# A one-layer hybrid encoder: query and key stores on ScalarE, fewer transfers of softmax statistics, operand sums on VectorE

## The chip, the cores and the metric

One Trainium2 chip, one of its cores. The metric is the device time of one execution in microseconds (us). Before the change three runs took 1313.45, 1315.63 and 1310.13 us, a median of 1313.45. A core has a matrix engine (TensorE, in the profile PE, with its weight loads as PEld), three engines for elementwise work (VectorE = DVE, ScalarE = ACT, GpSimd = POOL) and SyncE (SP), which here issues all transfers. Each engine works through its own list of instructions in order.

## The reference

One layer over x of 1024 positions by 1024 features, and 256 memory tokens, in float32. With `h = rms_norm(x)`, a single projection makes queries, keys and values of 8 heads of 64, a gated convolution input and the queries of 4 memory heads:

```python
q, k, v, glu, qm = split(rms_norm(x) @ w_in)
# group A: windows (128,1), (512,4), (2048,16): width and stride of the keys,
#          each normalised, then combined by the softmax of their log-sum-exps
# group B: GLU, depthwise convolution over 31, layer norm, silu
# group C: attention of qm to 256 memory tokens
h = x + concat(A, B, C) @ w_out
f = depthwise_conv3(rms_norm(h) @ w_up)          # 2 x 2816 columns
out = h + (silu(f_gate) * f_up) @ w_down
```

## The kernel before, in words

**Numbers.** A float32 operand is split into a high and a low part that TensorE takes (`hi`, `lo`); a product is three passes, hi*hi, hi*lo and lo*hi. ScalarE copies the high part, VectorE or GpSimd subtracts to get the low part.

**Stages of the span.** Until about 560 us the input projection (L917), the heads, the convolution, the memory heads and the output projection (L1099) run interleaved; from 562 to 622 the second norm, which also turns its rows into operands of the FFN's up projection; to 1064 the up projection in 22 pairs of column blocks, by a Strassen-like scheme with seven products over operands named A11, A12, A22, S1 to S4; to the end the down projection (L1334).

**Order of the work.** The program is written as generators (`Steps`) whose parts are started and advanced in turn; tiles come from pools with few buffers (`st.new`, `st.free`), and a scheduler with a model of the times sets the order of each engine's list. So an edit in one place can move rows elsewhere.

**Queries and keys.** `heads` (L829 on) takes a projected block of 128 positions by 256 columns out of PSUM (`raw`, L832, ScalarE), squares it (L833), norms it, splits it (`hl`, L864), has TensorE turn it (L871), copies it out of PSUM on ScalarE (`out`, L875) and stores it to DRAM through SP (L877): `qk_d` 32 times, the memory heads' `qm_d` 8 and `km_d` 2 times, 256 KB each. `values` (L884 to L890) stores the values in two orders, `v_d` by position (L888) and `vr_d` by class (L890). `head` (L338 on) loads `qk` (L346 to L349) and v (L393, L394) from there.

**Statistics.** Each head has two groups of scores: the near window, in which a block of 128 queries starts 64 positions late (so the last block wraps around, `qe`), and the class group, whose queries are gathered by position mod 64 into classes (`qc`), with masks m2a and m2b. For each query and group there is a maximum and a sum (`stat`, `stat2`). To combine the groups, `softmax_weights` brings the class group's statistics into the near group's order through DRAM: 8 stores to `st_d` (L299), 4 loads (L303 to L306), then weights on GpSimd and ScalarE, a turn on TensorE, and 4 stores to `w_d` (L336, L337); `weigh` loads the weights as rows, spread over 64 partitions (`wt`, L468), multiplies, adds and splits.

**Mixed parts.** The split result of each of the 8 column blocks of the mixed heads (k = 0 to 3 the heads, 4 and 5 the convolution, 6 and 7 memory) is kept in SBUF when its place is there (`mx`, `mx_more`, `mx_last`), and otherwise goes from `mx_part` to DRAM (`m_d`, L229) and back (L1085). Which of these it is depends on the moment at which the part is made: `room_for` (L206 on). The output projection takes the parts in the rounds 0, then 4 and 5, then 1, 2, 6, then 3 and 7. Convolution parts are made at L1024 (ScalarE) and L1026 (VectorE).

**The second norm.** `norm(t)` takes the eight row tiles of 128. VectorE scales (L1173, two halves). For tiles 4 to 7 the halves of tile t - 4 (`low0`, `low1`) and of tile t (`high0`, `high1`) are combined in place: `high1 = high0 + high1` on GpSimd (L1183, gives S1), `high0 = low0 - high0` (L1184, S3) and `low0 = high1 - low0` (L1185, S2) on VectorE, `low1 = low1 - low0` on GpSimd (L1189, S4). `turn_rows` turns each on TensorE (L1159, `ps_n`), copies the high part on ScalarE (L1161) and subtracts for the low part on VectorE (L1162). The FFN's first weights are loaded, summed (L1221) and split (L1207, L1208) at the same time, mostly on GpSimd. The first product of the up projection is `ps_d` at L1226.

Of the kernel before, what the change touches and what calls it, by code (L numbers as in the profile page):

```python
# [9 lines left out]
F = mybir.dt.float32  # L10
R = mybir.dt.float32r
I32 = mybir.dt.int32
AF = mybir.ActivationFunctionType
OP = mybir.AluOpType
# [4 lines left out]
S, D = 1024, 1024  # L19
# [24 lines left out]
def constants():  # L44


    c = {}
    n = np.arange(S)
# [9 lines left out]
    m2 = np.where(in4 & in16, twice, np.where(in4 | in16, np.float32(0), neg)).astype(np.float32)  # L58
    c["m2a"], c["m2b"] = m2[0:128], m2[128:256]
# [73 lines left out]
def block(tc, a, out):  # L133
# [3 lines left out]
    def f32(ap):  # L137
        return ap.bitcast(F)
# [38 lines left out]
    w_d = [dpool.tile([1, 2, S + 64], F, name=f"w_d{h}") for h in range(8)]  # L177
# [111 lines left out]
    def split_mixed(k, parts, src, cut=slice(None)):  # L289
        hi, lo = (t[:, cut] for t in parts)  # L290
        act.activation(natural(hi), classed(src), AF.Copy)
        yield
        dve.tensor_tensor(natural(lo), classed(src), f32(natural(hi)), OP.subtract)

    def softmax_weights(h, stat, stat2):


        for k in range(8):
            sp.dma_start(st_d[h][k].rearrange("(r s) c n -> s r (c n)", r=4),  # L299
                         stat2[16 * k : 16 * k + 16].rearrange("s r c n -> s r (c n)"))  # L300
        yield
        there = stat[:, 1].rearrange("p u c n -> p u (c n)")
        sp.dma_start(there[0:64], st_d[h][1:8:2].rearrange("k p c n -> p k (c n)"))  # L303
        sp.dma_start(there[64:128, 0:3], st_d[h][2:7:2].rearrange("k p c n -> p k (c n)"))
        for c in range(2):
            sp.dma_start(stat[64:128, 1, 3, c], st_d[h][0, :, 1 - c])  # L306
# [28 lines left out]
        for g in range(2):  # L335
            sp.dma_start(w_d[h][0, g, 64 : S + 64].rearrange("(u p) -> u p", p=128), rows[8 * g : 8 * g + 8])  # L336
            sp.dma_start(w_d[h][:, g, 0:64], rows[8 * g + 7 : 8 * g + 8, 64:128])  # L337
        count(("w", h))  # L338

    def head(h):  # L340
# [9 lines left out]
        for _ in range(3):  # L350
# [5 lines left out]
        pool.tensor_scalar(qc.rearrange("p r (k s) -> p r k s", s=16),  # L356
                           f32(q).rearrange("p (k r s) -> p r k s", r=4, s=16), 1.0, 0.0, OP.mult, OP.add)
# [43 lines left out]
        def evacuate(ps, j):  # L401

            other = yield from st.new("other", [128, 512])
            out, more = us[j // 2][to : to + 64], other[to : to + 64]
            if j < 2:
                n = 512 if j == 0 else 448
                views = [(out[:, 512 * j + 64 : 512 * j + 64 + n], ps[:, 0:n], more[:, 0:n])]
                if j:
                    views.append((out[:, 0:64], ps[:, 448:512], more[:, 448:512]))
            else:  # L410
                out = out.rearrange("p (k r s) -> p r k s", r=4, s=16)[:, 2 * j - 4 : 2 * j - 2]
                views = [(out, *(t.rearrange("p (r k s) -> p r k s", r=2, s=16) for t in (ps, more)))]
            act.activation(more, ps[frm : frm + 64], AF.Copy)
            for o, p, _ in views:
                act.activation(o, p[to : to + 64], AF.Copy)
            st.free("o")
            yield
            for o, _, m in views:
                pool.tensor_tensor(o, o, m, OP.add)
            st.free("other")  # L420
            count(("u", h))
            yield
# [33 lines left out]
    def weigh(p):  # L456
# [19 lines left out]
        for half in range(2):  # L476
# [10 lines left out]
            yield from split_mixed(p, parts, us[0][:, cut], cut)  # L487
# [73 lines left out]
    with tc.tile_pool(name="p1", bufs=1, side="right") as p1:  # L561
# [266 lines left out]
        def heads(ps, g, keys, rot, dst, key):  # L828
# [48 lines left out]
            sp.dma_start(dst, f32(t))  # L877
# [286 lines left out]
    def norm(t):  # L1164
# [18 lines left out]
        pool.tensor_tensor(high1, high0, high1, OP.add)  # L1183
# [5 lines left out]
        pool.tensor_tensor(low1, low1, low0, OP.subtract)  # L1189
# [177 lines left out]
```

## Time and profile before

| | us |
|---|---|
| runs (median of three) | 1313.45 |
| the profiled execution's own time | 1310.28 |
| its span | 1308.5 |
| TensorE busy | 1197.1 |
| VectorE, GpSimd, ScalarE busy | 868.7, 788.5, 626.6 |
| mean granted TensorE clock (of full speed) | 0.963 |

How to read its lines. A page gives busy time by engine, and the span in 40 slices of 32.7 us, a digit for each (tenths, 9 is 90% or more). A row of the timeline is start, duration, engine, line and operation with what it writes and reads, and in brackets the idle time of the engine ahead of it and what released it. A row of waits is who waited at which line, for what: us in total, times, longest. A row of the chain (start, duration, what) is a piece of the work that ended last, followed back. A row of a line's groups ends with minimum/median/maximum in ns and the first and last start in us. SPq is SP's queue, that is, the issuing of transfers, which isn't counted as busy time.

### The profile page before, as it was taken

To read this page: it belongs to the slowest core of one execution; us is meant where nothing else is said; L and a number is where in the kernel's file an instruction comes from. 1 tells how busy PE (TensorE), PEld (TensorE's weight loads), DVE (VectorE), ACT (ScalarE), POOL (GpSimd) and SP (SyncE) were. 2 spreads that over 40 slices of the span, in tenths; PEclk is the share of its full clock that TensorE was granted. 3 is DMA by queue.
4 is the path that set the end of the run, shared out by engine and by line. 5 is a ranking of instruction groups with operands and counts; after the bars stand their busy time and mean duration, and the time that the engine had idled before them with its cause. 6 is when DMAs were issued, how large, how long until landed. Compare 5 with 4: busy or idle time off the path is not lost.

```text
span 1308.5 us, 18556 instructions
## 1 busy us (share of the span) xinstructions
PE 1197.1 (91%) x6287; PEld 1000.3 (76%) x6287; DVE 868.7 (66%) x1272; ACT 626.6 (48%) x1296; POOL 788.5 (60%) x793
## 2 busy tenths in 40 slices
PE   4899988799988898885999999999999999999997
PEld 3887887799877786563877777777777788888886
DVE  6748879676685786887487778778787762224222
ACT  5664165468766576553344444344444443333331
POOL 4835286498894454367466667676676745555552
PEclk9999988999989898896999999999999999999999
DMA  7353525566575622161122222222222254448443
GB/s 253 112 170 100 159 82 161 169 180 178 144 252 164 188 74 78 28 213 49 34 87 81 65 86 67 81 89 65 89 71 83 81 175 155 145 145 272 146 146 120
DMA packets 166555, 164.81 MB, mean 126 GB/s; under 512 B 20322, under 2 KB 125756, under 8 KB 166460
## 3 DMA queue, kind: packets, MB, share of 16 engines
q1 hardware_dynamic: 166460, 163.63, 40.3%
q8 instruction: 49, 0.80, 0.3%
q14 instruction: 46, 0.38, 0.1%
HBM read 121.51 MB, written 42.08 MB: 125 GB/s over the span
## 4 chain that ended last, share of the span: by engine, by line
PE 46%; DVE 18%; issue 8%; ACT 7%; POOL 6%; DMA 5%; SPq 1%; POOLq 0%; ACTq 0%; DVEq 0%
PE ps_dn L1334 18%; PE ps_c L1226 6%; PE ps_d L1226 6%; PE proj L1099 4%; PE proj L917 3%; DVE yg L1295 3%; DVE conv L980 2%; DVE yu L1295 2%; PE o L287 2%; DMA v<-vr_d 2%; POOL up_lo L1208 2%; PE turn L278 2%; PE ps_a L1226 2%; ACT yu L1293 2%; DVE yg L1294 1%
## 5 line engine op out<-in xcount | busy, mean ns | idle before, releaser
L917 PE MATMUL proj<-w_hi,hnT 128*128 128x256 f32 x896 | 188.1, 298 | 23.7 <-ACT raw L832 12.9
L1208 POOL TENSOR_TENSOR up_lo<-dn_raw,up_hi 128x512 fp32r<-128x512 f32 x88 | 131.7, 1517 | 114.1 <-ACT up_hi L1207 111.3
L1208 POOL TENSOR_TENSOR up_lo<-up_sum,up_hi 128x512 fp32r<-128x512 f32 x88 | 154.8, 1768 | 55.8 <-PE ps_c L1226 22.7
L917 PEld LDWEIGHTS proj<-w_hi,hnT 128*128 128x128 f32 x896 | 150.9, 200 | 27.9 <-ACT raw L832 14.1
L1208 POOL TENSOR_TENSOR up_lo<-up_raw,up_hi 128x512 fp32r<-128x512 f32 x66 | 116.0, 1760 | 68.8 <-PE ps_a L1226 46.3
L1208 DVE TENSOR_TENSOR up_lo<-dn_raw,up_hi 128x512 fp32r<-128x512 f32 x44 | 57.6, 1311 | 147.5 <-ACT up_hi L1207 141.4
L1207 ACT ACTIVATE up_hi<-dn_raw 128x512 fp32r<-128x512 f32 x132 | 75.1, 623 | 161.4 <-issue 118.8
L1334 PE MATMUL ps_dn<-up_lo,up_hi 128*128 128x512 f32 x352 | 136.8, 389 | 0.0
L1334 PE MATMUL ps_dn<-up_hi,up_lo 128*128 128x512 f32 x352 | 136.3, 389 | 0.0
L1334 PE MATMUL ps_dn<-up_hi 128*128 128x512 f32 x352 | 134.7, 389 | 0.0
L917 PE MATMUL proj<-w_lo,hnT 128*128 128x256 f32 x448 | 131.9, 294 | 0.0
L1226 PE MATMUL ps_c<-S,up_hi 128*128 128x512 f32 x352 | 113.5, 404 | 6.6 <-ACT p L1278 6.6
L1226 PE MATMUL ps_a<-A,up_hi 128*128 128x512 f32 x352 | 111.1, 396 | 0.0
L636 POOL TENSOR_TENSOR w_lo<-w_raw,w_hi 128x512 fp32r<-128x512 f32 x44 | 62.8, 1437 | 59.4 <-ACT w_hi L634 58.8
L1221 DVE TENSOR_TENSOR up_sum<-up_raw,up_sum 128x512 f32<-128x512 f32 x40 | 59.0, 1476 | 50.4 <-POOL up_lo L1208 50.4
L917 PEld LDWEIGHTS proj<-w_lo,hnT 128*128 128x128 f32 x448 | 89.7, 200 | 0.5 <-POOL w_lo L624 0.4
L980 DVE SCALAR_TENSOR_TENSOR conv<-conv,cwT 128x1009 f32<-128x1009 f32 (+14 forms) x60 | 89.3, 1488 | 0.8
L1226 PEld LDWEIGHTS ps_c<-S,up_hi 128*128 128x128 f32 x352 | 65.4, 190 | 28.3 <-ACT p L1278 13.6
L1111 DVE TENSOR_TENSOR x<-proj,x 128x512 f32<-128x512 f32 x96 | 64.1, 682 | 25.0 <-PE proj L1099 24.9
L1293 ACT ACTIVATE yu<-cu,fwT 128x1024 f32<-128x1024 f32 x22 | 27.4, 1244 | 108.0 <-DVE cu L1286 106.3
L1226 PEld LDWEIGHTS ps_a<-A,up_hi 128*128 128x128 f32 x352 | 65.8, 188 | 15.8
L1334 PEld LDWEIGHTS ps_dn<-up_lo,up_hi 128*128 128x128 f32 x352 | 66.1, 188 | 13.8
(240 smaller groups left out, 3150.2 us busy)
## 6 DMA issues: line engine op xcount, KB each, us to landing
up_raw<-w_up SPq DMA_DIRECT2D x92, 256.0 KB
dn_raw<-w_down SPq DMA_DIRECT2D x88, 256.0 KB
g_d<-yg SPq DMA_DIRECT2D x22, 512.0 KB
dn_raw<-g_d SPq DMA_DIRECT2D x44, 256.0 KB
x<-x SPq DMA_DIRECT2D x16, 512.0 KB
qk_d<-out SPq DMA_DIRECT2D x32, 256.0 KB
qk<-qk_d SPq DMA_DIRECT2D x16, 512.0 KB
w_raw<-w_in SPq DMA_DIRECT2D x40, 128.0 KB
```

What stands on the lines that cost most here:

```text
L636: (dve if next(chunk_no) < EARLY else pool).tensor_tensor(lo, raw, f32(hi), OP.subtract)
L917: pe.matmul(ps[:, :256], lhs[i][:, k], c.parts[k][j], start=(k == 0 and i == 0 and j == 0), stop=(k == KT - 1 and i == 1))
L980: dve.scalar_tensor_tensor(acc[:, c0:c1], conv_in[i][:, c0 + k - 15 : c1 + k - 15], w, acc[:, c0:c1], OP.mult, OP.add)
L1099: pe.matmul(ps, mixed[k][i][:, 128 * t : 128 * t + 128], wo[k, half][j], start=(n == 0), stop=(n == 3 * len(ks) - 1))
L1111: dve.tensor_tensor(dst, ps, dst, OP.add)
L1207: act.activation(hi, src, AF.Copy)
L1208: adder.tensor_tensor(lo, src, f32(hi), OP.subtract)
L1221: adder.tensor_tensor(t, x, y, OP.subtract)
L1226: pe.matmul(ps, w[i][:, k], ops[x][j][:, k], start=(first and n == 0), stop=(n == 3 * KH - 1), skip_group_check=not first)
L1293: act.activation(y, c, AF.Identity, scale=tap[1], bias=b)
L1295: dve.scalar_tensor_tensor(y[:, 0 : S - 1], c[:, 1:S], tap[2], y[:, 0 : S - 1], OP.mult, OP.add)
L1334: pe.matmul(ps, gk[i][:, 128 * t : 128 * t + 128], wk[half][j], start=(k == 0 and m == 0), stop=(k == NF - 1 and m == 2))
```

## The change

- **Stores of queries and keys.** All 42 stores of L877 are issued by ScalarE, behind its copy out of PSUM (new line L872), instead of SP.
- **Statistics.** The class group's queries are gathered from 16 positions on (the mask is rolled by 16 and `qc` is written in two pieces), so that its blocks and the near group's have the same order in DRAM. A head's statistics go out in 4 transfers instead of 8 and come back in 1 instead of 4; the weights in 1 instead of 4. The near group's sum `u` is kept in the late order (no pieces of 448 and 64 in `evacuate`), and `weigh` shifts it when it splits, its second half in pieces of 448 and 64.
- **Operand sums.** L1183 and L1189 go from GpSimd to VectorE (new lines L1178 and L1184), eight operations of 128x512.

In all 737 transfers become 661; SP issues 118 fewer rows. TensorE's order is the same over its first 450 matmuls and its last 2556. As a side effect of the new times in the scheduler's model the convolution part k = 4 now goes to `mx_part` and through `m_d` (two more stores of 512 KB and two more loads), where it went straight to `mx` before.

The diff:

```diff
-    w_d = [dpool.tile([1, 2, S + 64], F, name=f"w_d{h}") for h in range(8)]
+    w_d = [dpool.tile([1, 2, S], F, name=f"w_d{h}") for h in range(8)]
...
+    m2 = np.roll(m2, -16, axis=0)
...
     def softmax_weights(h, stat, stat2):
-        for k in range(8):
-            sp.dma_start(st_d[h][k].rearrange("(r s) c n -> s r (c n)", r=4),
-                         stat2[16 * k : 16 * k + 16].rearrange("s r c n -> s r (c n)"))
-        yield
-        there = stat[:, 1].rearrange("p u c n -> p u (c n)")
-        sp.dma_start(there[0:64], st_d[h][1:8:2].rearrange("k p c n -> p k (c n)"))
-        sp.dma_start(there[64:128, 0:3], st_d[h][2:7:2].rearrange("k p c n -> p k (c n)"))
-        for c in range(2):
-            sp.dma_start(stat[64:128, 1, 3, c], st_d[h][0, :, 1 - c])
+        for r in range(4):
+            sp.dma_start(st_d[h][:, 16 * r : 16 * r + 16].rearrange("k s c n -> k s (c n)"),
+                         stat2[:, r].rearrange("p c n -> p (c n)"))
+        yield
+        sp.dma_start(stat[:, 1].rearrange("p u c n -> p u (c n)"),
+                     st_d[h].rearrange("(u e) p c n -> (e p) u (c n)", e=2))
...
-        for g in range(2):
-            sp.dma_start(w_d[h][0, g, 64 : S + 64].rearrange("(u p) -> u p", p=128), rows[8 * g : 8 * g + 8])
-            sp.dma_start(w_d[h][:, g, 0:64], rows[8 * g + 7 : 8 * g + 8, 64:128])
+        sp.dma_start(w_d[h][0].rearrange("g (u p) -> (g u) p", p=128), rows)
...
-        pool.tensor_scalar(qc.rearrange("p r (k s) -> p r k s", s=16),
-                           f32(q).rearrange("p (k r s) -> p r k s", r=4, s=16), 1.0, 0.0, OP.mult, OP.add)
+        to_c, from_q = qc.rearrange("p r (k s) -> p r k s", s=16), f32(q).rearrange("p (k r s) -> p r k s", r=4, s=16)
+        for k0, k1, n in ((0, 1, 15), (15, 0, 1)):
+            pool.tensor_scalar(to_c[:, :, k0 : k0 + n], from_q[:, :, k1 : k1 + n], 1.0, 0.0, OP.mult, OP.add)
...
-            yield from split_mixed(p, parts, us[0][:, cut], cut)
+            for n0, n1 in (((0, 512),) if not half else ((512, 960), (960, 1024))):
+                dst = (n0 + 64) % S
+                yield from split_mixed(p, parts, us[0][:, n0:n1], slice(dst, dst + n1 - n0))
...
             act.activation(t, f32(pt), AF.Copy)
             st.free("turn", "out")
-            sp.dma_start(dst, f32(t))
+            act.dma_start(dst, f32(t))
...
-        pool.tensor_tensor(high1, high0, high1, OP.add)
+        dve.tensor_tensor(high1, high0, high1, OP.add)
         dve.tensor_tensor(high0, low0, high0, OP.subtract)
         dve.tensor_tensor(low0, high1, low0, OP.subtract)
...
-        pool.tensor_tensor(low1, low1, low0, OP.subtract)
+        dve.tensor_tensor(low1, low1, low0, OP.subtract)
```

What moves in the engines' lists. First SP's list around the stores of head 1's weights (`w_d_87`), where the trace stands near 240 to 253 us; `vr_d_73` and `v_d_71` are the values, `wt` the weights' loads, `w_raw` the projection's. Before:

```order
L888 DMA v_d_71<-out 128x512
L890 DMA vr_d_73<-out 4x16x512 x2
L336 DMA w_d_87<-rows 8x128
L337 DMA w_d_87<-rows 1x64
L336 DMA w_d_87<-rows 8x128
L337 DMA w_d_87<-rows 1x64
L468 DMA wt<-w_d_87 64x512
L888 DMA v_d_71<-out 128x512
L468 DMA wt<-w_d_87 64x512
L890 DMA vr_d_73<-out 4x16x512 x2
L595 DMA w_raw<-w_in 128x2x256 x2
```

And after:

```order
L883 DMA v_d_71<-out 128x512
L885 DMA vr_d_73<-out 4x16x512 x2
L333 DMA w_d_87<-rows 16x128
L883 DMA v_d_71<-out 128x512
L885 DMA vr_d_73<-out 4x16x512
L461 DMA wt<-w_d_87 64x512 x2
L885 DMA vr_d_73<-out 4x16x512
L590 DMA w_raw<-w_in 128x2x256 x2
```

One store stands where four stood; the next block of values has moved ahead of the weights' first reader.

Next VectorE's list in the second norm. `x_4994` and `x_4995` are tiles 6 and 7, `x_4992` and `x_4993` tiles 4 and 5, `x_4988` and `x_4989` tiles 0 and 1. Before:

```order
L1173 SCALAR_TENSOR_TENSOR x_4994<-x_4994,ss_7000,g_ffn_7001 128x512
L1173 SCALAR_TENSOR_TENSOR x_4994<-x_4994,ss_7000,g_ffn_7002 128x512
L1162 TENSOR_TENSOR A_6993<-ps_n,A_6992 128x4x128
L1184 TENSOR_TENSOR x_4992<-x_4988,x_4992 128x512
L1185 TENSOR_TENSOR x_4988<-x_4992,x_4988 128x512
L1173 SCALAR_TENSOR_TENSOR x_4995<-x_4995,ss_7000,g_ffn_7001 128x512
L1173 SCALAR_TENSOR_TENSOR x_4995<-x_4995,ss_7000,g_ffn_7002 128x512
L1162 TENSOR_TENSOR S_6995<-ps_n,S_6994 128x4x128
L1162 TENSOR_TENSOR S_6999<-ps_n,S_6998 128x4x128
L1162 TENSOR_TENSOR S_6997<-ps_n,S_6996 128x4x128
L1162 TENSOR_TENSOR A_6993<-ps_n,A_6992 128x4x128
L1184 TENSOR_TENSOR x_4993<-x_4989,x_4993 128x512
```

After, with tile 7 as `x_5126`, tiles 4 and 5 as `x_5123` and `x_5124`, tiles 0 and 1 as `x_5119` and `x_5120`:

```order
L1178 TENSOR_TENSOR x_5123<-x_5123 128x512
L1157 TENSOR_TENSOR A_6919<-ps_n,A_6918 128x4x128
L1179 TENSOR_TENSOR x_5123<-x_5119,x_5123 128x512
L1180 TENSOR_TENSOR x_5119<-x_5123,x_5119 128x512
L1168 SCALAR_TENSOR_TENSOR x_5126<-x_5126,ss_6926,g_ffn_6927 128x512
L1168 SCALAR_TENSOR_TENSOR x_5126<-x_5126,ss_6926,g_ffn_6928 128x512
L1184 TENSOR_TENSOR x_5119<-x_5119 128x512
L1157 TENSOR_TENSOR S_6921<-ps_n,S_6920 128x4x128
L1157 TENSOR_TENSOR S_6925<-ps_n,S_6924 128x4x128
L1178 TENSOR_TENSOR x_5124<-x_5124 128x512
L1179 TENSOR_TENSOR x_5124<-x_5120,x_5124 128x512
L1157 TENSOR_TENSOR S_6923<-ps_n,S_6922 128x4x128
```

The sums L1178 and L1184 have come in, and tile 5's difference (L1179) now stands two rows of copies earlier than L1184 did.

Last ScalarE's list where the memory queries are made (before, near 310 us):

```order
L875 ACTIVATE out<-turn 128x512
L864 ACTIVATE hl<-raw 128x4x64
L833 ACTIVATE sq<-raw 128x256
L875 ACTIVATE out<-turn 128x512
L864 ACTIVATE hl<-raw 128x4x64
L240 ACTIVATE prob,stat<-prob,stat 128x256 x2
```

And after:

```order
L870 ACTIVATE out<-turn 128x512
L859 ACTIVATE hl<-raw 128x4x64
L872 DMA qm_d<-out 512x1x128
L241 ACTIVATE prob,stat<-prob,stat 128x256
L870 ACTIVATE out<-turn 128x512
L859 ACTIVATE hl<-raw 128x4x64
L241 ACTIVATE prob,stat<-prob,stat 128x256
```

The store stands one to seven rows behind the copy that makes its data, with the exponentials of a head (L241) behind it.

More of the change, by code (lines that the diff above doesn't have):

```diff
@@ L405, in evacuate @@
             if j < 2:
[L406 to L409, printed above, removed]
+                out = out[:, 512 * j : 512 * j + 512]
+                here = ps
             else:
                 out = out.rearrange("p (k r s) -> p r k s", r=4, s=16)[:, 2 * j - 4 : 2 * j - 2]
[L412 to L415, printed above, removed]
+                here, more = (t.rearrange("p (r k s) -> p r k s", r=2, s=16) for t in (ps, more))
+            act.activation(more, here[frm : frm + 64], AF.Copy)
+            act.activation(out, here[to : to + 64], AF.Copy)
             st.free("o")
             yield
-            for o, _, m in views:
-                pool.tensor_tensor(o, o, m, OP.add)
+            pool.tensor_tensor(out, out, more, OP.add)
             st.free("other")
```

## The prediction

> **What bounds the kernel now.** I read the page first, for where the engines are full and where not.
>
> ```profile
> PE 1197.1 (91%) x6287; PEld 1000.3 (76%) x6287; DVE 868.7 (66%) x1272; ACT 626.6 (48%) x1296; POOL 788.5 (60%) x793
> PE   4899988799988898885999999999999999999997
> PEclk9999988999989898896999999999999999999999
> PE 46%; DVE 18%; issue 8%; ACT 7%; POOL 6%; DMA 5%; SPq 1%; POOLq 0%; ACTq 0%; DVEq 0%
> ```
>
> TensorE is busy for 91% of the span, and from slice 20 on (654 us) nearly always. The change touches nothing behind there, so what can be won lies in the slices below 9, which are stretches of the first 622 us. The last line is the chain that ended last: TensorE carries 46% of it, ScalarE only 7%, transfers 5%, SP's issuing 1%. I then asked for the busy time of those stretches.
>
> ```profile
> 200.00:258.00 58.00, 44.22 (x345) 42.94 (x343) 46.16 (x78) 27.49 (x71) 28.11 (x35) 0.90 0.57 170
> 300.00:360.00 60.00, 56.86 (x473) 54.34 (x471) 40.09 (x116) 48.61 (x136) 47.51 (x79) 1.00 0.59 164
> 360.00:410.00 50.00, 41.96 (x248) 35.23 (x249) 39.01 (x93) 39.73 (x96) 38.73 (x66) 0.93 0.74 236
> 585.00:622.00 37.00, 21.47 (x94) 15.74 (x93) 27.48 (x29) 14.10 (x24) 27.95 (x22) 0.67 0.16 49
> ```
>
> The columns behind the length are the busy us of TensorE, its weight loads, VectorE, ScalarE and GpSimd, then granted clock, DMA share and GB/s. The poorest stretch is 585 to 622 us, the second norm: TensorE idles 15.5 of 37 us. From 200 to 258 it idles 13.8 us. From 300 to 360, where the memory queries are made, it idles 3.1 us, and ScalarE has 11.4 us left.
>
> **Operand sums on VectorE (the norm).** The waits between 560 and 625 us, then TensorE, GpSimd and VectorE on the timeline:
>
> ```profile
> PE ps_n L1159 <- POOL x L1183: 6.8, 2, 5.4
> PE ps_n L1159 <- DVE x L1184: 5.2, 2, 4.5
> 601.51 1.12 PE L1159 MATMUL ps_n<-identr,x 128*128 128x128 f32 x4 [5.42 <-POOL x L1183]
> 607.08 1.09 PE L1159 MATMUL ps_n<-identr,x 128*128 128x128 f32 x4 [4.45 <-DVE x L1184]
> 598.97 1.27 POOL L1221 TENSOR_TENSOR up_sum<-up_raw,up_sum 128x512 f32<-128x512 f32 x1
> 600.20 1.26 POOL L1183 TENSOR_TENSOR x<-x 128x512 f32<-128x512 f32 x1
> 590.69 3.49 DVE L1173 SCALAR_TENSOR_TENSOR x<-x,ss,g_ffn 128x512 f32<-128x512 f32 x2 [1.69 <-POOL ss L165]
> 594.11 1.27 DVE L1162 TENSOR_TENSOR S<-ps_n,S 128x512 fp32r<-128x512 f32 x2
> 596.77 0.68 DVE L1162 TENSOR_TENSOR A<-ps_n,A 128x512 fp32r<-128x512 f32 x1
> 601.49 5.44 DVE L1184 TENSOR_TENSOR x<-x,x 128x512 f32<-128x512 f32 x1 [4.04 <-POOL x L1183]
> L1184 DVE TENSOR_TENSOR x<-x,x x4: 673/936/5444, 587.1 to 619.1; 128x512 f32<-128x512 f32 x4
> 621.81 1.22 PE L1226 MATMUL ps_d<-S,up_hi 128*128 128x512 f32 x2 [0.69 <-ACT S L1161]
> ```
>
> One tile costs most. Its sum L1183 stands on GpSimd behind the operand sums of the FFN weights (L1221 is one) and starts at 600.20; VectorE idles 4.04 us for it, TensorE 5.42. Then L1184 on VectorE takes 5.44 us where the median of four is 0.94, and TensorE idles 4.45 more. The stage ends with the first ps_d, at 621.81.
>
> The trace has no L1183 on VectorE. The nearest row is L1184, the same shape: 0.67 at best, 0.94 median, 5.44 at worst; I take the median. With the new order VectorE does, from 594.18 on: L1184 of the tile before 0.94, two copies from PSUM 1.27, L1178 0.94, done near 597.4 instead of 601.5. L1179 then ends near 598.3 instead of 606.9. So the tile itself comes 4 to 8.5 us earlier. What is late next is VectorE: it is busy 27.48 us here, gains three L1178 and four L1184 (7 times 0.94, 6.6) and loses the stretch of the one long row (5.44 less 0.94, 4.5), which makes 29.6. A stage of 29.6 instead of 37.0 is 7.4 less, if VectorE never waits; with two of its waits of about 1 us (1.69 for ss is quoted) **5.5 us** stay. Best end: all waits for both lines go, 6.8 and 5.2, 12 us less. Worst: one of the seven stretches as L1184 did, 4.5 more than reckoned, and the gain is 1, or a loss of 2 with two stretched.
>
> The Trainium skill ("GPSIMD Engine Reference", 1. Specifications) says that GpSimd shares its SBUF interfaces with VectorE and that instructions with two SBUF inputs contend for them. The 5.44 us row, beside GpSimd at work without a break, agrees with it; it would speak for the worst end, since the moved sums are of that kind.
>
> **Fewer statistics transfers, stores off SP.** Per head 16 transfers become 6, for eight heads 80 fewer; 42 stores go to ScalarE's queue. What this frees on SP matters only where a load behind them is waited for. On SP, ScalarE and TensorE around 250 us:
>
> ```profile
> 240.43 0.30 SPq L336 DMA_DIRECT2D w_d<-rows  x1
> 243.43 0.21 SPq L337 DMA_DIRECT2D w_d<-rows  x1
> 248.00 0.51 SPq L468 DMA_DIRECT2D wt<-w_d  x1
> 250.99 2.21 SPq L595 DMA_DIRECT2D w_raw<-w_in  x2
> 257.02 0.63 ACT L634 ACTIVATE w_hi<-w_raw 128x512 fp32r<-128x512 f32 x1 [8.64 <-DMA w_raw<-w_in]
> 258.11 0.58 PE L917 MATMUL proj<-w_hi,hnT 128*128 128x256 f32 x1 [5.59 <-ACT raw L832]
> ```
>
> Four stores of one head's weights go out between 240.43 and 243.43, their first reader at 248.00, and the projection's weights behind it at 250.99; 7.1 us later TensorE ends an idle of 5.59. With one store at about 240.4 the reader could go 3 us earlier. In the new order, though, stores of values stand between, and one of them is ready only near 247; so the weights gain 1.3 to 3 us. I take **2** (ends 0 and 5.6, the whole idle).
>
> ```profile
> SPq L877 <- ACT hl L864: 28.0, 6, 13.3
> SPq L877 <- ACT out L875: 18.5, 8, 9.5
> 401.64 9.60 DMA v<-vr_d
> 445.92 7.02 DMA v<-vr_d
> PE o L287 <- DMA v<-vr_d: 4.4, 3, 2.9
> 290.16 3.82 DMA w_raw<-w_in
> ```
>
> Ahead of L877 SP's queue itself stood still 46.5 us, for ScalarE's copies, with loads behind. Those two loads of v lie on the chain, and TensorE idled 4.4 us for v in all. If they go out a few transfers earlier I take half of it, **2** (ends 0 and 4.4). Of the load at 290.16, also on the chain, and all others, 1.5 of its 3.82 us, ends 0 and 3.8. SP together: **5.5 us less**.
>
> The new order of classed queries costs GpSimd eight tiny copies and saves eight; the half that is split costs four small instructions each on ScalarE and VectorE; both engines have slack in all rows above: nothing.
>
> **The stores on ScalarE.** What one costs there the trace shows on SP only:
>
> ```profile
> L877 SPq DMA_DIRECT2D qk_d<-out x32: 512/536/645, 47.9 to 419.2; - x32
> L877 SPq DMA_DIRECT2D qm_d<-out x8: 524/558/1430, 312.9 to 353.7; - x8
> SPq L299 <- DMA x<-x: 4.7, 5, 1.0
> 301.08 3.61 SPq L299 DMA_DIRECT2D st_d<-stat  x8
> ```
>
> 42 times 0.54 is 22.5 us of ScalarE time, 4% more. The 8 qm stores and two of qk fall into 300 to 360 us, 5.4 us against 11.4 free. ScalarE is busy 626.6 us and carries 7% of the chain, 91.6 us, about 15% of its time; 15% of 22.5 is **3.3 us**. Ends: 0, all hidden in ScalarE's half-empty time, and 22.5, none.
>
> The Trainium skill ("DMA: Bandwidth & Descriptors", Issuing engines are not separate DMA queues) says that issuing from a second engine saves only the sequencer's time for the issue, usually small beside the transfer. L299's eight issues at 3.61 us agree that an issue is 0.45 us; by the rule alone, the 5.5 us would shrink to about nothing (second rival).
>
> **The detour of a convolution part.** As a side effect of the timing, the first of the two convolution parts no longer goes straight to its last place, but through DRAM, like the heads: two more stores and two more loads of 0.5 MB.
>
> ```profile
> 404.62 1.04 ACT L1024 ACTIVATE mx_more<-conv 128x1024 fp32r<-128x1024 f32 x1
> 405.72 0.50 PE L1099 MATMUL proj<-w_hi,mx_more 128*128 128x512 f32 x1 [0.95 <-ACT mx_more L1024]
> ```
>
> Today TensorE waits 0.95 us there for the second part. The convolution's norm now stands earlier: between its last transpose and that matmul lie 26.8 us of TensorE work (estimated from the trace's durations of the same rows), 11.7 before. A store and a load at the rate of those of v (9.60 and 7.02) need some 17 us. So **0**, ends 0 and 10, the latter with both transfers under the 236 GB/s of the stretch 360 to 410.
>
> **Sum.** The profiled execution took 1310.28 us, its span 1308.5 and 1.8 around it. 5.5 and 5.5 less, 3.3 more: 7.7 less, 1302.6. That execution lies 3.17 below the median of the runs (1313.45), so **1305.8 us**. A measurement of this kernel can tell about 0.5% from no change: faster is below 1306.9, slower above 1320.0.
>
> **Rivals.**
>
> *ScalarE is the one that waits.* SP's stores waited not only for their producers: L299 waited five times, 0.9 us each, for loads of x, earlier transfers that are nothing to it. In the built program 29 of the 42 stores on ScalarE likewise wait for the landing of an earlier transfer. ScalarE is in order, and behind a waiting store stand the copies that empty PSUM for the projection (L832, L875) and the exponentials. At 0.54 and 0.94 a store costs 1.5 us, 10 of them in 300 to 360 us make 15 against 11.4 free; 42 make 62 us, and with a third on the path 21 more, against 11 less: 1313.45 plus 10, **1323**. It decides from a third on the path; the chain's 15% speaks against, the full TensorE (56.86 of 60) in that stretch for it.
>
> *SP's relief is worth nothing.* The loads wait for the landing of w_d and for the values' stores, which stay on SP, and v's 9.60 us are transfer. Then 5.5 less, 3.3 more: 1313.45 less 2.2, **1311**, within 0.5%. For it: that store of values near 247.
>
> *The detour is late.* At its end of 10 us: 1305.8 plus 10, **1316**. Against it: the 26.8 us of cover.
>
> That the change does not do what it says can be excluded for the counts: the order shows 118 fewer transfers on SP.
>
> **Chances.** Forecast 0.52, ScalarE waits 0.18, relief worth nothing 0.22, detour late 0.08. The forecast's own range is 1296 to 1311 (norm at 12 and ScalarE free; or norm at 1, ScalarE as reckoned); about three quarters of it lie below 1306.9, that is 0.40. Faster: these and 0.05 of the second rival, 0.45. Slower: 0.16 of the first rival and 0.01 of the third, 0.17. The same: 0.38. The range goes from 1292 (norm 12, the weights at 250 us 5.6, v 4.4 less, ScalarE free: 22.0) to 1321, which leaves out the upper half of the first rival.
>
> **What would show it.** In the profile after: L1178 near 597 with TensorE's wait before S1 under 2 us, the first ps_d before 617 (still 621.81, with the same start, would mean that VectorE took the gain); the idle of 5.59 near 256 shortened; no ScalarE copy that waits behind a store by over 1 us between 300 and 360; mx_more landed ahead of its matmul. Wrong if VectorE's sums take over 2 us, or if ScalarE's busy rows in 300 to 360 spread while TensorE falls below 54.

## The result, and the profile after

The changed kernel took 1320.0 us (median of 7), the kernel before 1310.13 beside it: a ratio of 1.0065 over all runs (not of the two medians), 95% interval 1.0035 to 1.0094. Measured again with other kernels beside it, it was 1.0071 (1.0046 to 1.0097). It is slower by 0.7%, where 1305.8 and "faster" were forecast.

The page of the kernel after, the same lines as before:

```profile
PE 1197.1 (91%) x6287; PEld 999.2 (76%) x6287; DVE 865.6 (66%) x1284; ACT 626.9 (48%) x1292; POOL 782.1 (59%) x785
PE   4899888899776989786999999999999999999997
PEclk9999988999897999898899999999999999999999
PE 39%; DVE 20%; DMA 9%; ACT 8%; issue 7%; POOL 5%; SPq 1%; ACTq 0%; POOLq 0%; DVEq 0%
```

TensorE is busy for the same 1197.1 us. Counted from 0, its slices 7, 13, 15 and 18 (the norm) are fuller, and 4, 10 to 12, 14 and 16 emptier. Transfers have grown on the chain from 5 to 9%. The busy time by stretch, after, then of two of them before:

```profile
200.00:300.00 100.00, 88.08 (x688) 86.28 (x687) 78.97 (x156) 60.09 (x159) 75.27 (x110) 0.91 0.61 174
300.00:400.00 100.00, 80.28 (x628) 75.70 (x627) 59.84 (x175) 78.52 (x209) 68.58 (x118) 0.92 0.55 163
400.00:500.00 100.00, 85.21 (x461) 69.48 (x461) 66.70 (x165) 51.81 (x136) 51.02 (x72) 0.93 0.61 174
594.00:631.00 37.00, 25.12 (x112) 18.33 (x111) 34.38 (x40) 15.28 (x27) 22.69 (x16) 0.75 0.18 57
```

```profile
200.00:300.00 100.00, 84.64 (x662) 82.41 (x661) 77.18 (x151) 57.25 (x155) 68.80 (x103) 0.91 0.58 170
300.00:400.00 100.00, 90.55 (x676) 83.42 (x675) 71.18 (x197) 78.84 (x214) 78.59 (x136) 0.97 0.62 187
```

Up to 300 us the change gains: 3.4 us more TensorE work are done between 200 and 300. Between 300 and 400 it does 10.3 us less. The whole difference is best cut at two matmuls that every kernel has, the first `ps_n` (the second norm starts) and the first `ps_d` (the up projection's first full stage). In the kernel after:

```profile
574.21 0.52 PE L1154 MATMUL ps_n<-identr,x 128*128 128x128 f32 x3 [2.87 <-DVE x L1168]
630.81 0.78 PE L1221 MATMUL ps_d<-S,up_hi 128*128 128x512 f32 x1
```

The norm starts at 574.2 instead of 562.2 (12.0 later), takes 56.6 us instead of 59.6 (3.0 less), and the rest, from there to the end of the last matmul, is 1.1 less: 7.9 of the 8.2 us by which the spans differ (1316.7 and 1308.5). So the loss lies ahead of 574 us, and the norm's gain is there, at half its size.

The widest idle of TensorE between 200 us and that point stands at 406.66 (two wider ones, 7.7 at 12 and 6.3 at 169, have like ones in the kernel before, 7.8 and 5.5). On the timelines of ScalarE and TensorE, then on the chain:

```profile
397.17 0.52 ACTq L872 DMA_DIRECT2D qk_d<-out  x1
399.83 0.21 ACT L316 ACTIVATE w<-w 128x16 f32<-128x16 f32 x1
405.66 0.52 ACTq L872 DMA_DIRECT2D qk_d<-out  x1
406.22 0.38 ACT L827 ACTIVATE raw<-proj 128x256 f32<-128x256 f32 x1 [6.19 <-DMA m_d<-mx_part]
406.66 0.80 PE L1094 MATMUL proj<-w_hi,mx 128*128 128x512 f32 x1 [5.93 <-ACT raw L827]
```

```profile
394.59 10.99 DMA m_d<-mx_part
```

This is the first rival at its plainest, joined to the third: the detour's store of the convolution part takes 10.99 us, a store of keys on ScalarE waits for its landing, and behind it stands the copy that TensorE needs. The stretches around it (busy times as above, then clock, DMA share, GB/s):

```profile
380.00:390.00 10.00, 7.34 (x64) 7.20 (x63) 5.26 (x23) 9.92 (x26) 2.36 (x9) 1.00 0.25 57
390.00:395.00 5.00, 3.06 (x13) 2.58 (x13) 2.72 (x3) 4.97 (x10) 4.72 (x4) 0.55 1.03 419
395.00:400.00 5.00, 2.73 (x9) 1.93 (x10) 2.70 (x4) 4.95 (x14) 0.47 (x2) 0.50 1.03 383
400.00:405.00 5.00, 0.73 (x2) 0.01 (x1) 0.00 (x0) 0.04 (x1) 1.68 (x4) 0.50 1.02 363
```

The transfer engines are full, and the granted clock is 0.50. It had fallen before this wait: TensorE idled 4.2 us up to 391.5, and the clock, 1.00 until 390, is 0.55 in the next five us. The Trainium skill ("TensorE: Matmul & The Clock Gate", Part 1) says that the clock falls to half after about 3.4 us without work; these rows agree. A wait thus costs more than its own length: a 128x512 matmul of this line takes 0.80 us at 406.66, and one took 0.50 at 405.72 in the kernel before, where the clock from 405 to 410 was 1.00.

### The profile page after: what moved, and what is told of

The parts are those of the page before. It is cut to its first block, busy times and chain, and to the rows that moved or that the text cites. A ratio compares the mean times of both kernels' runs of the same rounds, so it can differ in the third digit from the quotient of the medians.

```text
span 1316.7 us, 18480 instructions
## 1 busy us (share of the span) xinstructions
PE 1197.1 (91%) x6287; PEld 999.2 (76%) x6287; DVE 865.6 (66%) x1284; ACT 626.9 (48%) x1292; POOL 782.1 (59%) x785
## 4 chain that ended last, share of the span: by engine, by line
PE 39%; DVE 20%; DMA 9%; ACT 8%; issue 7%; POOL 5%; SPq 1%; ACTq 0%; POOLq 0%; DVEq 0%
PE ps_dn L1329 17%; PE ps_c L1221 5%; PE ps_d L1221 5%; DVE yg L1290 3%; DVE conv L975 3%; DVE yu L1290 3%; PE proj L1094 2%; PE proj L912 2%; POOL up_lo L1203 2%; DVE yg L1289 2%; DVE yu L1289 2%; ACT yu L1288 2%; PE o L288 2%; DMA qk<-qk_d 2%; DMA v<-vr_d 1%
## 5 line engine op out<-in xcount | busy, mean ns | idle before, releaser
L1216 DVE TENSOR_TENSOR up_sum<-up_raw,up_sum 128x512 f32<-128x512 f32 x40 | 56.2, 1405 | 50.6 <-POOL up_lo L1203 50.6
L1288 ACT ACTIVATE yu<-cu,fwT 128x1024 f32<-128x1024 f32 x22 | 27.4, 1244 | 112.2 <-DVE cu L1281 111.8
L1329 PEld LDWEIGHTS ps_dn<-up_lo,up_hi 128*128 128x128 f32 x352 | 66.1, 188 | 14.9 <-POOL up_lo L1203 1.2
```

Of the source, the lines that this page charges most:

```text
L1216: adder.tensor_tensor(t, x, y, OP.subtract)
L1288: act.activation(y, c, AF.Identity, scale=tap[1], bias=b)
L1329: pe.matmul(ps, gk[i][:, 128 * t : 128 * t + 128], wk[half][j], start=(k == 0 and m == 0), stop=(k == NF - 1 and m == 2))
```

## The experiments

The first theories were three. **A**: ScalarE's waiting store is the loss. **B**: the new order of TensorE's list is, in which the heads come earlier and the projections later. **C**: the detour's 2 MB are. Some of the expectations below also speak of **D** (the statistics part is sound, its loss is the detour), **F** (the detour costs beside the rest of the change in any order), **G** (it costs because the part comes late) and **I** (it costs by its transfers and the list order that they bring). "Norm starts" is the first `ps_n` of each one's profile, and "rest" goes from the first `ps_d` to the end of the last matmul. "Tail" lies ahead of the norm, from the start of the 257th matmul of the output projection to that of the 273rd. "Run" is by how much the profiled execution lay above (+) or below (-) the median of its kernel's runs (for the kernel before, of all 109). All but the ratio are us.

| | edit | ratio to before (95%) | run | norm starts | tail | norm stage | rest |
|---|---|---|---|---|---|---|---|
| before | | 1 | -2.3 | 562.2 | 36.1 | 59.6 | 678.9 |
| after | | 1.0065 (1.0035 to 1.0094) | -1.5 | 574.2 | 31.7 | 56.6 | 677.8 |
| e5 | after, again | 1.0071 (1.0046 to 1.0097) | +1.7 | 581.3 | 31.0 | 57.2 | 677.6 |
| e1 | after, 8 stores on SP | 1.0006 (0.9989 to 1.0022) | +1.7 | 572.1 | 31.6 | 56.6 | 677.2 |
| e2 | after, no detour | 0.9932 (0.9909 to 0.9956) | +1.3 | 563.6 | 24.7 | 56.5 | 677.8 |
| e8 | both | 0.9942 (0.9921 to 0.9962) | +2.6 | 563.6 | 24.9 | 57.0 | 678.1 |
| e3 | before, sums on VectorE | 0.9964 (0.9947 to 0.9981) | -2.5 | 562.6 | 35.8 | 56.5 | 678.3 |
| e4 | before, stores on ScalarE | 1.0014 (0.9997 to 1.0031) | -3.6 | 564.8 | 36.1 | 59.5 | 678.1 |
| e6 | before, detour | 1.0003 (0.9989 to 1.0018) | -3.2 | 564.0 | 25.3 | 57.6 | 679.3 |
| e7 | statistics alone | 1.0082 (1.0055 to 1.0108) | -0.5 | 575.5 | 34.5 | 57.5 | 679.6 |
| e9 | statistics, no detour | 0.9914 (0.9897 to 0.9932) | +0.5 | 563.6 | 22.8 | 58.8 | 668.7 |
| e15 | after, all stores on SP | 0.9978 (0.9958 to 0.9998) | +0.8 | 576.8 | 33.2 | 56.6 | 668.7 |
| e12 | the same, no detour | 0.9918 (0.9900 to 0.9936) | -4.3 | 561.9 | 22.8 | 56.2 | 669.2 |
| e10 | after, head 4 held | 0.9872 (0.9852 to 0.9893) | +2.1 | 562.6 | 16.2 | 57.2 | 668.7 |
| e11 | the same, detour | 0.9957 (0.9940 to 0.9975) | +1.0 | 571.2 | 27.4 | 56.5 | 669.0 |
| e13 | e10, stores on SP | 0.9937 (0.9915 to 0.9959) | +0.2 | 560.0 | 26.0 | 56.6 | 678.2 |
| e14 | e9, 2 MB of idle transfers | 1.0061 (1.0037 to 1.0086) | +3.8 | 574.5 | 31.3 | 60.2 | 680.2 |
| e16 | e9, 32 KB of idle transfers | 0.9949 (0.9928 to 0.9970) | -0.8 | 568.1 | 26.0 | 58.4 | 668.2 |

A profile is one execution: after and e5 are the same kernel, and the norm starts 7 us apart. Differences of 2 us in one pair of profiles prove nothing; the pattern over many pairs does. So where a price ahead of the norm matters, a second figure is given, "by the times": the difference of the two ratios, as us of 1312.5, less what the columns "norm stage" and "rest" account for. The intervals make that good to about 4 us.

**The waiting store (e1, e2, e8).** e1 gives the last eight qk stores back to SP; TensorE's list stays the same row for row.

```diff
-            act.dma_start(dst, f32(t))
+            (sp if key == ("qk", 3) else act).dma_start(dst, f32(t))
```

> The changed kernel, with the eight qk stores of the last pair of heads issued by SP again; TensorE's order is that of the changed kernel, row for row. Theory A (ScalarE stands 6.2 us near 400 us at a store that waits for the landing of another transfer, and the projection's copies behind it hold TensorE for 5.9): about 6 us less than the changed kernel, 1314, and no ScalarE idle over 2 us ahead of L827 between 395 and 410. Rival B (the new order of TensorE's list costs the time, ScalarE's wait only fills it) and rival C (the detour's 2 MB crowd the other loads between 390 and 412): 1319 to 1321 as the changed kernel, with the TensorE idle of 5.9 moved to another releaser.

ScalarE in e1, at the place where it stood for 6.2 us:

```profile
403.05 0.36 ACT L827 ACTIVATE raw<-proj 128x256 f32<-128x256 f32 x1
403.32 0.20 ACT L316 ACTIVATE w<-w 128x16 f32<-128x16 f32 x1
403.42 0.37 ACT L827 ACTIVATE raw<-proj 128x256 f32<-128x256 f32 x1
572.13 0.58 PE L1154 MATMUL ps_n<-identr,x 128*128 128x128 f32 x2 [2.93 <-DVE x L1168]
```

The wait is gone. Matmul by matmul, e1 is 3.5 us behind the changed kernel just ahead of the place and 2.2 ahead of it just behind, a gain of 5.7 as theory A has it; but it had lost the 3.5 before, and 2.1 remain at the norm. The measured gain of 0.6% (8 us, between two comparisons whose intervals do not overlap) fits A. The traces show less of it, since the changed kernel's profiled execution was one of its quicker ones and e1's one of its slower ones. e2 takes the detour away and keeps the stores:

```diff
+                    while not keeping:
+                        yield
                     parts = yield from new_mixed(4 + i)
```

> The changed kernel, with the convolution part k = 4 made only when its place in SBUF is there, so that it does not go through DRAM. Theory A: the transfer that ScalarE's store waited for is gone, 1314. Rival C (the 2 MB themselves): 1310 to 1314, with the loads between 390 and 412 landing earlier. Rival B: 1319 to 1321, with TensorE's idle at 349 (4.8 us, behind the convolution's norm) and 391 (4.2 us) as in the changed kernel and a new wait at the first matmul of the part.

It falls by 1.3% below the changed kernel (17 us), nearly three times what A asks, and by more than C's 6 to 10; the idles at 349 and 391 that speak for B are still there in its trace (4.1 and 4.2 us), so they are not the loss. Both edits at once (e8) should have shown A once more, since in e2 ScalarE still waits behind a store (for a load of mixed parts), and TensorE 4.11 us for ScalarE:

```profile
402.77 0.52 ACTq L872 DMA_DIRECT2D qk_d<-out  x1
403.39 0.59 ACT L408 ACTIVATE other<-o 64x512 f32<-64x512 f32 x1 [3.45 <-DMA mx<-m_d]
```

> The changed kernel without the detour and with the last pair's qk stores on SP, which joins the first two edits. In the trace without the detour ScalarE still idles 3.45 us behind its store, for another landing, and TensorE 4.1 us. Theory A: these 3 to 4 us go as well, 1.0 to 1.2% below before, about 1300 beside 1313. Rivals B and C: no less than without the detour alone, 0.7% below before.

In e8 both of these idles are gone, and the norm starts at 563.6 as in e2; the time is the same. Here A fails: without the detour the wait was real, and taking it away gained nothing.

**The parts alone (e3, e4, e7), and the changed kernel as a measure (e5).**

> The kernel before, with only the sums L1183 and L1189 on VectorE. The prediction's term: 5.5 us less than before, 1304.6. By the changed kernel's trace the stage from the first ps_n to the first ps_d is 56.6 us instead of 59.6: 3 less, 1307. If VectorE gives back what it wins: 1310.

> The kernel before, with only the 42 stores on ScalarE. The prediction's term: 3.3 us more for the issue, less up to 5.5 for what SP is rid of, 1308 to 1313. Theory A in general (ScalarE's stores wait for landings and hold the copies behind them): 1316 or more, with ScalarE idle ahead of copies behind a store. Rival B and C put the loss elsewhere (the statistics part): 1310 or below.

> The changed kernel with its stores on SP and its sums on GpSimd again: the fewer transfers of statistics alone, with the detour that comes with them. The prediction's term: up to 5.5 us less than before. Theory A: no ScalarE store can wait, so at most the detour's own price, within 3 us of before. Theory B (the new order of TensorE, which comes with the statistics): 6 us or more above before. Theory C: 5 to 10 us above before.

> The changed kernel itself, beside the next three on one chip, as their measure: 0.3 to 0.9% slower than before, as in the result. All theories agree.

The sums give 0.36% (4.7 us of time; 3.1 us of the norm stage in the trace). The stores alone cost nothing that the interval can tell. The statistics part alone, with stores on SP, is 0.82% slower, against A, for B or C. That part also brings the detour.

**The detour, in the old order and in the new (e6, e9, e12, e15).** In the kernel before, e6 sends the part through DRAM by force:

```diff
-        if not keeping:
+        if not keeping or k == 4:
             return "mx_part"
```

> The kernel before, with only the convolution part k = 4 sent through DRAM (two stores and two loads of 512 KB more), stores on SP. Theory C (the 2 MB themselves cost, by late parts and crowded loads): 5 to 10 us more than before. Theory A (the detour costs only because a store on ScalarE waits for its landing): within 2 us of before. Theory B: within 2 us of before.

No cost, against C. But with the statistics part the same detour decides whether there is a loss (e9 has e2's edit):

> The statistics part alone (stores on SP, sums on GpSimd), with the convolution part k = 4 made only when its place in SBUF is there. Theory D (the statistics part is sound, and its loss is the detour that the new order brings): 0.3 to 0.7% less than before, 1304 to 1309 beside 1313. Theory B (TensorE's new order itself, with the projections 10 us of work later, costs): 0.4% or more above before, 1318.

> The changed kernel without the detour and with all 42 stores on SP again: statistics and sums. Theory A (stores on ScalarE cost by their waits): 2 to 4 us less than the changed kernel without the detour, 0.9% below before. If the stores' own cost is nil: 0.6 to 0.8% below before. If SP is relieved by them: 0.5% or less below before.

> The changed kernel with all 42 stores on SP, detour kept. Theory A (the loss is ScalarE's store that waits for the detour's landing): 0.1% above before or less, as with the last pair's stores on SP. Theories G and I (the detour costs without ScalarE): 0.4 to 0.6% above before, that is 1.3% over the same kernel without the detour.

By the norm's start: e9 563.6 against e7 575.5; e12 561.9 against e15 576.8; e2 563.6 against after 574.2. The detour costs 11 to 15 us there, **with and without stores on ScalarE**. Chance is a small part of it: TensorE's list up to the norm is the same, row for row, in e7 and e15, and in e9 and e12, and within each two the starts differ by under 2 us. By the times the detour costs 11 (e7), 8 (e15) and 17 us (after).

So A falls as the only cause: without ScalarE's stores the detour costs too. As a part of the changed kernel's loss A is not excluded: e1, which rids ScalarE of its wait, gained 8 us, while e15, with all stores on SP, gains against the changed kernel only 2 to 3 us by the times beside what the up loop's order brings (below). B, that the earlier heads and later projections of the new order cost by themselves, falls: e2, e9 and e12 keep the statistics part, and their norm starts within 1.5 us of before's.

**What in the detour costs (e11, e14, e16).** e14 keeps the part in SBUF for TensorE, and adds four transfers that nobody needs at the same place of the program:

```diff
                     finish_mixed(4 + i, parts)
                     count("conv_parts")
+                    if i == 0:
+                        for n, t in enumerate(parts):
+                            sp.dma_start(m_d[:, 4, n], f32(t))
+                        again = yield from st.several(2, "mx_part", [128, S], R)
+                        for n, t in enumerate(again):
+                            sp.dma_start(f32(t), m_d[:, 4, n])
+                        st.free("mx_part", "mx_part")
```

> The statistics part alone without the detour, with four transfers of 512 KB added that nobody needs: the convolution part k = 4 is stored from its place and loaded into a free buffer, at the same place of the program. TensorE uses the part in SBUF. Theory G (the detour costs because the part comes late): no loss, 0.7 to 0.9% below before. Theory I (the transfers cost, by crowding SP and the loads behind them, and by the order of the last heads, which the scheduler now puts 5 to 10 us of TensorE work later): most of the 1.7% comes back, 0.3 to 0.9% above before.

The norm starts at 574.5, as with the detour. So the transfers cost although no part comes late, and G falls as the only cause; by the times they cost 8 us, and up to a few us of lateness beside them are not excluded. (Of e14's total over e9, 1.5%, more than half arises behind the norm, in the up loop.) e16 cuts the four transfers to a 64th:

> The statistics part alone without the detour, with the four needless transfers cut to 16 of 1024 columns (8 KB each). In TensorE's list head 6 now ends after 351 us of work, where it is 347 without the transfers and 357 with the full ones; the up loop has the quick order, as without them. Theory I-order (the place of the last heads costs): the norm starts about 4 us later than the 563.6 without the transfers, near 568, against 574.5 with the full ones; total 0.5% below before. Theory I-bytes (2 MB crowd the loads): the norm starts at 563 to 565, total 0.8% below before.

It starts at 568.1, where the list order's reckoning had put it, not at 563 to 565: transfers of 8 KB can hardly crowd others, yet they cost 4.5 us, 5 by the times, which cannot be told from e14's 8. What they change is the list: the scheduler, which gives each transfer a place and a time in its model, puts the last heads later in TensorE's list (by that reckoning head 6 ends after 347 us of work in e9, 351 in e16, 357 in e14). One sees it in the tail, between the 257th and the 273rd matmul of the output projection, when little but the last heads and the memory heads is left. e9, e16 and e14:

```profile
519.20:542.00 22.80, 17.77 (x92) 12.30 (x92) 19.62 (x44) 16.25 (x37) 10.79 (x12) 0.97 0.07 24
```

```profile
521.00:546.90 25.90, 19.55 (x97) 13.68 (x96) 19.45 (x43) 17.60 (x40) 13.40 (x16) 0.93 0.09 31
```

```profile
521.70:553.10 31.40, 24.04 (x121) 17.97 (x120) 22.68 (x57) 21.26 (x50) 15.50 (x18) 0.87 0.07 26
```

At its start they are within 2.5 us of each other; then the tail takes 22.8, 25.9 and 31.4, since 92, 97 and 121 matmuls are still to be done there, in a chain of scores, exponentials and turns, with idle between and a clock that falls from 0.97 to 0.87. Of e14's 10.9 us over e9, 8.6 arise here; of e16's 4.5, 3.1. The detour itself does the same, as the table's column shows: the tail takes 34.5 us in e7 against 22.8 in e9, 33.2 in e15 against 22.8 in e12, 31.7 in the changed kernel against 24.7 in e2. That is 11.7 of 11.9 us, 10.4 of 14.9 and 7.1 of 10.6, and the tail starts no earlier for it (0.8, 4.4 and 4.0 us later); the rows below count 120 matmuls there in the changed kernel and 96 in e2. In the kernel before, the tail is worse still. That is why a forced detour was free there: e6 lost at the place of the part (the 49th matmul of the output projection at 418.4 instead of 400.9), and its tail takes 25.3 us instead of 36.1. The rows of before, after and e2:

```profile
504.50:540.60 36.10, 26.88 (x123) 20.04 (x122) 23.20 (x55) 22.62 (x53) 16.85 (x21) 0.76 0.07 22
521.50:553.20 31.70, 24.00 (x120) 18.00 (x119) 22.53 (x57) 21.24 (x50) 15.36 (x18) 0.86 0.08 26
517.50:542.20 24.70, 18.36 (x96) 13.13 (x96) 19.89 (x45) 16.85 (x38) 12.68 (x13) 0.96 0.07 22
```

The last of these experiments holds head 4 back until the memory queries are stored, so that the projection's last matmul stands where it was before; the convolution part then finds its place by itself (e10). e11 adds the detour to it, e13 gives the stores to SP.

```diff
         while stored.get(("qk", p), 0) < NT:
             yield
+        while h == 4 and stored.get("qm", 0) < NT:
+            yield
```

> The changed kernel, with head 4 held back until the memory queries are stored: the projection's last matmul stands where it stood before (after 314 us of TensorE work instead of 325), and the convolution part finds its place, so there is no detour. Theory D: as without the detour, 0.5 to 0.9% less than before. Theory B: the order's own loss goes as well, 1.2% or more less than before, 1297.

> As the kernel with the head held back, but with the convolution part k = 4 sent through DRAM by force (it is loaded again into a buffer of its old kind). Theory D (the detour costs only where its store falls among the residual's and the mixed parts' loads): within 0.4% of the kernel with the head held back. Rival F (2 MB more cost wherever the rest of the change is in): 1.0 to 1.4% above it.

> The changed kernel with head 4 held back (no detour) and all 42 stores on SP. If the stores on ScalarE cost 2 us by themselves, as their single run and the pair without the detour hint: 1.3 to 1.5% below before. If ScalarE's issue frees SP for loads that matter in this order: 1.0 to 1.2% below before.

e10 is the best of all, 1295.94 us against 1311.02 before, 1.3% less. e11 loses 8.6 us at the norm to it, 11.2 of it in the tail (27.4 us against 16.2) with 2.4 won ahead of that, so the detour is not free there either. 0.85% was measured: D's bound (0.4%) is missed, and F's (1.0 to 1.4%) too, though its lower end lies within what the two intervals leave.

**A second order that no part of the change is about.** The column "rest" knows two values only, 677 to 680 and 668 to 669. The up loop's list comes out in one of two ways, and which of them depends on edits far ahead of it. The loop from 720 to 780 us in the kernel after, then in e10:

```profile
720.00:780.00 60.00, 59.18 (x249) 46.16 (x249) 47.59 (x39) 25.30 (x38) 41.26 (x24) 1.00 0.25 79
```

```profile
720.00:780.00 60.00, 60.00 (x259) 48.17 (x258) 48.44 (x43) 29.35 (x43) 42.58 (x25) 1.00 0.27 84
```

259 matmuls against 249 in the same time, and no idle. In the quick list the first two matmuls of `ps_b` stand ahead of those of `ps_a`, and the other ten behind them; in the slow one each product's twelve stand together. The waits show only a part of it, here in the kernel before from 700 to 1050 us:

```profile
PE ps_c L1226 <- ACT p L1278: 3.7, 15, 0.3
```

The quick list is worth about 9 us, 0.7%, in e9, e10, e11, e12, e15 and e16, and this must be taken out before their ratios are compared, which the expectations for e10, e12, e13 and e14 did not foresee: of e10's 1.3%, 0.7 come from here, and what is left is D's forecast and not B's; e13's stores on SP do not cost 0.65% but fell to the slow list (its norm starts 2.6 us earlier than e10's). e15 is "faster than before" for this reason alone.

## Why the prediction was wrong

- **What bounds the kernel**: right. Only the first 622 us were in question, and TensorE's work did not change.
- **Operand sums on VectorE**: the right way, mis-sized. 5.5 us were forecast, 3.0 to 3.1 measured in the norm stage (0.36% of time, e3); in the new order it is 0.9 (e15 against e7) and 2.6 (e12 against e9). TensorE's waits of 5.42 and 4.45 became these:

```profile
611.93 0.69 PE L1154 MATMUL ps_n<-identr,x 128*128 128x128 f32 x4 [3.47 <-DVE S L1157]
616.46 1.09 PE L1154 MATMUL ps_n<-identr,x 128*128 128x128 f32 x4 [3.84 <-DVE A L1157]
```

And on VectorE, on the timeline and for the sum's line:

```profile
609.49 1.64 DVE L1179 TENSOR_TENSOR x<-x,x 128x512 f32<-128x512 f32 x1
612.31 1.74 DVE L1216 TENSOR_TENSOR up_sum<-up_raw 128x512 f32<-128x512 f32 x1 [0.52 <-POOL up_lo L1203]
613.97 1.75 DVE L1180 TENSOR_TENSOR x<-x,x 128x512 f32<-128x512 f32 x1
```

```profile
L1178 DVE TENSOR_TENSOR x<-x x4: 679/686/959, 598.3 to 626.7; 128x512 f32<-128x512 f32 x4
```

VectorE is late next, as said; it is busy for 34.38 of the last 37 us. The price taken for L1178 (0.94) was too high, its median is 0.69; but its neighbours stretch to 1.6 to 1.8 us, and the weight sums on VectorE (L1216), three as before, now take up to 1.74 us where the longest took 1.47.
- **SP's relief**: the step that was local came true. The idle of 5.59 at 258 is gone, and from 200 to 300 us 3.4 us more work is done. At the norm it cannot be found in the traces: e9, with this part and without the detour, starts it at 563.6, before at 562.2, and by the times e9 gains 0.3 us ahead of it. So 5.5 us less became about 0 there, as the second rival had it. (e2 and e8, which have the stores on ScalarE too, gain 4 to 5 by the times, about as much as the uncertainty.) That the earlier heads and projections were won in a list whose tail is bound by the last heads, and so were lost again, is an argument and not shown.
- **Stores on ScalarE**: an issue there takes 0.52 us, as on SP. The norm starts 2.6 us later with them in e4, 1.7 in e2 against e12, 2.6 in e10 against e13, where 3.3 were forecast; but with the detour the pair after and e15 gives -2.6 or, by e5, +4.5, and e4's time is 0.14% longer with an interval that reaches 0. So the size is neither confirmed nor refuted. The Trainium skill's rule ("DMA: Bandwidth & Descriptors", Issuing engines are not separate DMA queues), which the prediction cites, agrees with e4: issuing from a second engine gained nothing. The first rival's waits exist, but outside the stretch that it named: 6.19 us at 406, which with the detour cost up to 8 us (e1) and without it nothing (e8). Its 21 us are not there.
- **The detour**: the step that failed. "So **0**, ends 0 and 10": it costs 11 to 15 us at the norm's start, by the times 8 to 11 with all stores on SP and 17 in the changed kernel. It was priced as a wait for the part, with 26.8 us of cover, and e14, where TensorE has the part in SBUF and the transfers alone remain, pays most of the price all the same. By e16 and the tails, most of the price came by the place that four transfers take in the scheduler's model, which moves the last heads, and this the prediction had before it: it looked at the order at three places, and not at the order of the tail. In the changed kernel the wait of ScalarE for the detour's store comes on top, up to 8 us by e1.

Together: 12.0 us more ahead of the norm, 3.0 less in it, where the forecast had 5.5 less by relief, 3.3 more by stores, nothing by the detour and 5.5 less by the norm. e2 is the case that the prediction summed, the change without the detour, in the same up loop as before: 0.68% less (8.9 us, interval 5.8 to 11.9), where 7.7 less were forecast. With that one term at nothing the total was thus right; its parts were not (the norm 3 instead of 5.5), so there is luck in how well it fits.

Left open: how much of the full transfers' price (e14) is order and how much bytes, since e16 moves the list by 4 us of work and e14 by 10, and no run keeps the list while the bytes change; why the stretch ahead of the tail is no shorter where it has fewer matmuls to do; how much of the changed kernel's loss is ScalarE's wait; and what makes the scheduler choose between the two up loops.

## What to carry to other kernels

Where a scheduler sets the lists, an edit's largest effect can be the order of work that it does not touch: compare the whole list, its tail above all, before pricing the edit. Then cut each trace at two or three matmuls that all versions share, and compare stage by stage; a total here mixed causes of 2 to 15 us, one of which, the up loop's order, had nothing to do with the question. Look too at where each profiled execution lies among its kernel's runs: here it was up to 4.3 us off their median. And when a wait has been found, take it away in more than one version before believing it: the plainest one in this profile was worth 8 us in one kernel and nothing in another.

## What the runs showed of the hardware

- One execution of the same kernel can have the same idle time and still be 7 us later, with TensorE's matmuls taking longer at a lower mean clock: up to the norm its busy time was 481.87 in the kernel after and 489.27 in e5, its idle time 92.3 and 92.0, and the mean granted clock of the whole execution 0.963 and 0.957.

```profile
0.00:574.20 574.20, 481.87 (x3217) 431.18 (x3218) 404.93 (x877) 336.18 (x837) 335.71 (x503) 0.94 0.51 149
```

```profile
0.00:581.30 581.30, 489.27 (x3218) 438.18 (x3219) 405.56 (x877) 336.25 (x837) 334.55 (x503) 0.93 0.51 147
```

- A store that ScalarE issues can hold ScalarE until a transfer from SP has landed: by the profile's releaser it idled 6.19 us for one of 512 KB that took 10.99 with the transfer engines full, and with that store on SP (e1) the idle is gone.
